# Modulated input made k tile by k tile: shift and scale of one tile at a time, four products with w_glu following; the norm's sums on TensorE

## The chip, the cores and the metric

One core of one Trainium2 chip runs the whole program. The metric is the time of one execution on the device in microseconds, and a kernel's time is the median of its runs.

## What is computed

The reference is a two-part network over 512 tokens of width 1024; the change lies at its very beginning. There a condition vector `c` gives six modulation vectors, two of which shift and scale the normalised input:

```python
mod = jax.nn.silu(c) @ w_ada[l] + b_ada[l]                      # 1024 -> 6 x 1024
sh1, sc1, gt1, sh2, sc2, gt2 = jnp.split(mod, 6, axis=-1)
h = modulate(rmsnorm(x, g_norm1[l]), sh1, sc1)                  # x_norm * g * (1 + sc1) + sh1
z = h @ w_in                                                    # all projections of the mixer
u = glu_a * jax.nn.sigmoid(glu_b)                               # the first 2 x 512 columns of z
```

After it come two causal convolutions, a chunked recurrent mixer, a mixture of 32 experts, and a second block with a delta rule, attention and two feed-forward layers.

## The kernel before

All activations are kept transposed: eight k tiles of 128 features x 512 tokens. A dense product (`dense`, L129, L132, L135) multiplies fp32 values as two rounded parts: for each of the eight k tiles it issues three matmuls of 512 columns, high x high, high x low, low x high, so 24 for one tile of 128 outputs. Weights come in `raw` tiles of 1 MB (five buffers), each with two such output tiles; ScalarE rounds them (`whi`, L105) and VectorE subtracts to get the low part (`wlo`, L106).

At the start, `ada_first` computes the shift and scale parts of `mod`. SP loads the eight tiles of `xT` and eight `raw` tiles of `w_ada`. ScalarE squares the x tiles (L1110), GpSimd adds the squares (L1112), TensorE sums over the features by one set of one-column matmuls (L172), and 13 small VectorE steps (`rsqrt_steps`, L150 to L165) give the norm, which TensorE broadcasts (L196). VectorE multiplies the rows of `w_ada` with the entries of silu(c) and accumulates (L1077, L1079); TensorE sums the accumulators over the partitions (L1085). GpSimd multiplies x with the norm (L1131). Then the mixer makes each tile's high part (L1386, ScalarE) and low part (L1387, L1389, VectorE). `glu_conv` runs eight products with the four `w_glu` tiles, and the next part of the modulation, `ada(2)`, streams beside it: eight tiles of 512 KB through the pool `ada` of three buffers (L1097), accumulated in `acc`. After `w_glu` comes the narrow product with `w_if` (L277).

Each engine runs its instructions in order. Inside a `manual_schedule` the listed engines keep the order of the code; elsewhere a scheduler sets it. SP's order, that of the loads, is the code's here, where `merge` interleaves `glu_conv` and `ada(2)`. A load into a buffer still in use waits in SP's queue, and the loads behind it wait too.

## Time and profile before

| | |
|---|---|
| median of three runs | 2391.74 us (2390.03 to 2392.57) |
| the profiled execution: time, span | 2389.36 us, 2387.6 us |
| TensorE matmuls busy | 2269.1 us (95% of the span) |
| VectorE busy | 1698.2 us (71%) |
| ScalarE busy | 1179.8 us (49%) |
| GpSimd busy | 205.7 us (9%) |
| read from HBM | 365.85 MB |

A busy share is an average over the whole span; the ends of matmuls are modelled, so two of them may be shown to overlap. An engine's idle time before an instruction is listed with what ended it. What matters for a change at the start is where TensorE is idle there, and whether it is ever idle later.

### The profile page before, as it was taken

Reading aid. Unit: us, or ns where it says so; the run is one execution under the profiler, and the core shown is the slowest. Engines: PE = TensorE matmul, PEld = TensorE weight load, DVE = VectorE, ACT = ScalarE, POOL = GpSimd, SP = SyncE. Lnnn points to the kernel's source line nnn. Section 1 sums busy time; section 2 is a strip of 40 time slices with the busy share of each in tenths; the row PEclk is TensorE's granted clock in tenths of the full one; section 3 lists DMA queues with packets and bytes.
Section 4 is the critical chain, followed back from the end, with each engine's and each line's share of the span. In section 5 each row is a group of like instructions: output and inputs, shape, how many; then the busy total and the mean of one; then the engine's idle time right before and its main releaser. Section 6 shows DMA issues by size and latency. Waiting matters only on the chain.

```text
span 2387.6 us, 30070 instructions
## 1 busy us (share of the span) xinstructions
PE 2269.1 (95%) x11062; PEld 1816.8 (76%) x11062; DVE 1698.2 (71%) x2931; ACT 1179.8 (49%) x1921; POOL 205.7 (9%) x283
## 2 busy tenths in 40 slices
PE   3999999799999999969999999999999999999997
PEld 2787788687677676636888887888888888888886
DVE  7698874688888888756677766763765766763763
ACT  2253443578777777755444424442444664432441
POOL 4000100001001001311233310000000000000000
PEclk9999999899999999979999999999999999999998
DMA  7634143279999999961111112223222212223220
GB/s 280 245 115 141 36 150 124 96 270 364 360 363 360 361 364 362 380 265 54 54 54 36 36 54 89 95 72 125 92 72 75 89 54 89 95 73 124 95 73 36
DMA packets 63302, 374.26 MB, mean 157 GB/s; under 512 B 8880, under 2 KB 9264, under 8 KB 25264
## 3 DMA queue, kind: packets, MB, share of 16 engines
q1 hardware_dynamic: 60048, 367.97, 41.7%
q0 software_dynamic: 2816, 4.20, 0.5%
q8 instruction: 88, 1.44, 0.2%
q14 instruction: 62, 0.51, 0.1%
q10 hardware_dynamic: 288, 0.14, 0.0%
HBM read 365.85 MB, written 11.67 MB: 158 GB/s over the span
## 4 chain that ended last, share of the span: by engine, by line
PE 47%; DVE 4%; POOL 2%; ACT 2%; issue 1%; DMA 1%; SPq 0%; DVEq 0%; POOLq 0%; ACTq 0%
PE mm L135 13%; PE mm L132 13%; PE mm L129 13%; PE wk L1045 1%; POOL blk_x L712 1%; POOL blk_t L710 1%; PE wk L743 1%; PE wk L748 1%; ACT act L1012 0%; DMA act<-yd 0%; POOL act L714 0%; PE wk L993 0%; DVE act L303 0%; PE wk L1029 0%; PE wk L1994 0%
## 5 line engine op out<-in xcount | busy, mean ns | idle before, releaser
L105 ACT CAST whi<-raw 128x1024 fp32r<-128x1024 f32 (+1 forms) x597 | 596.5, 1020 | 656.9 <-PE mm L132 526.2
L106 DVE TENSOR_TENSOR wlo<-raw,whi 128x1024 fp32r<-128x1024 f32 (+1 forms) x596 | 697.7, 1185 | 211.9 <-ACT whi L105 205.2
L129 PE MATMUL mm<-act,whi 128*128 128x512 f32 x1968 | 781.0, 398 | 2.1 <-DVE res L472 1.2
L132 PE MATMUL mm<-act,whi 128*128 128x512 f32 x1968 | 779.3, 396 | 2.7 <-DVE act L1389 2.3
L135 PE MATMUL mm<-act,wlo 128*128 128x512 f32 x1968 | 779.0, 396 | 0.3 <-DVE wlo L106 0.3
L132 PEld LDWEIGHTS mm<-act,whi 128*128 128x128 f32 x1968 | 371.6, 189 | 81.9 <-DVE act L1389 4.7
L129 PEld LDWEIGHTS mm<-act,whi 128*128 128x128 f32 x1968 | 371.8, 189 | 80.4 <-ACT whi L105 2.7
L135 PEld LDWEIGHTS mm<-act,wlo 128*128 128x128 f32 x1968 | 371.3, 189 | 79.3 <-issue 3.4
L303 DVE SCALAR_TENSOR_TENSOR act<-act,vec,act 128x511 f32<-128x511 f32 (+2 forms) x272 | 205.1, 756 | 19.0 <-ACT act L298 12.4
L1770 PE MATMUL gu<-whi,act 128*128 128x512 f32 x520 | 174.0, 421 | 0.2 <-ACT whi L105 0.2
L1770 PE MATMUL gu<-wlo,act 128*128 128x512 f32 x456 | 152.7, 416 | 9.4 <-DVE wlo L106 5.7
L105 ACT CAST act<-act 128x512 fp32r<-128x512 f32 (+1 forms) x96 | 52.8, 557 | 150.1 <-DVE act L349 93.6
L340 DVE TENSOR_TENSOR act<-mm,act 128x512 f32<-128x512 f32 x88 | 60.4, 688 | 84.4 <-PE mm L135 84.0
L1770 PEld LDWEIGHTS gu<-whi,act 128*128 128x128 f32 x520 | 93.6, 189 | 30.2 <-issue 13.2
L1770 PEld LDWEIGHTS gu<-wlo,act 128*128 128x128 f32 x456 | 76.7, 188 | 49.7 <-DVE wlo L106 39.6
L1844 POOL DMA_INDIRECT yd<-y,lst x32 | 68.6, 2144 | 484.5 <-DVE y L1843 414.6
L1747 PEld LDWEIGHTS xg<-s,act 128*128 128x128 f32 x576 | 85.9, 194 | 12.1 <-ACT act L113 2.0
L1747 PE MATMUL xg<-s,act 128*128 128x256 f32 x576 | 89.0, 287 | 1.9 <-DVE s L1732 1.9
L1181 DVE SCALAR_TENSOR_TENSOR act<-act,dw_half,act 128x482 f32<-128x482 f32 (+14 forms) x120 | 89.0, 743 | 0.5
L106 DVE TENSOR_TENSOR act<-act,act 128x512 fp32r<-128x512 f32 (+1 forms) x96 | 58.8, 612 | 42.3 <-ACT act L105 42.3
L300 ACT ACTIVATE act<-act,vec 128x512 f32<-128x512 f32 x96 | 78.0, 814 | 12.1 <-DVE act L340 8.4
L1770 PE MATMUL py<-whi,act 128*128 128x512 f32 x168 | 66.7, 478 | 2.7 <-DVE y L1843 2.7
(551 smaller groups left out, 2570.5 us busy)
## 6 DMA issues: line engine op xcount, KB each, us to landing
raw<-in_w_gu_dram SPq DMA_DIRECT2D x128, 1024.0 KB, 7.4
raw<-in_w_dn_dram SPq DMA_DIRECT2D x64, 1024.0 KB, 7.2
raw<-in_f_up_dram SPq DMA_DIRECT2D x44, 1024.0 KB, 4.8
raw<-in_f_dn_dram SPq DMA_DIRECT2D x32, 704.0 KB, 4.1
ada<-in_w_ada_dram SPq DMA_DIRECT2D x32, 512.0 KB, 5.2
raw<-in_a_h_dram SPq DMA_DIRECT2D x16, 1024.0 KB, 4.9
raw<-in_w_ada_dram SPq DMA_DIRECT2D x8, 1024.0 KB, 9.6
raw<-in_w_glu_dram SPq DMA_DIRECT2D x4, 1024.0 KB, 7.5
```

The source lines that it names most:

```text
L105: self.nc.scalar.copy(out=hi, in_=src)
L106: self.nc.vector.tensor_tensor(out=lo, in0=src, in1=hi.bitcast(F32), op=ALU.subtract)
L129: mm(out=p, lhsT=wh[:, s], rhs=xh, start=first and k == 0, stop=False)
L132: mm(out=p, lhsT=wh[:, s], rhs=xl, start=False, stop=False)
L135: mm(out=p, lhsT=wl[:, s], rhs=xh, start=False, stop=last and k == n - 1)
L300: nc.scalar.activation(out=y, in_=z, func=ACTF.Identity, scale=taps[n - 1], bias=bias)
L303: nc.vector.scalar_tensor_tensor(out=y[:, s:], in0=z[:, :T - s], scalar=taps[j], in1=y[:, s:], op0=ALU.mult, op1=ALU.add)
L340: nc.vector.tensor_tensor(out=z, in0=p, in1=rb, op=ALU.mult)
L1181: nc.vector.scalar_tensor_tensor(out=y[:, s:], in0=u[:, :T - s], scalar=taps[:, j, i:i + 1], in1=y[:, s:], op0=ALU.mult, op1=ALU.add)
L1747: nc.tensor.matmul(out=p[:, :n * r], lhsT=hT[k // 4][i][e][:, (k % 4) * 128:(k % 4) * 128 + 128], rhs=s[:, i, :n * r], start=i + e == 0, s ...
L1770: self.nc.tensor.matmul(out=o, lhsT=x, rhs=y[:, i * T:(i + 1) * T], start=first and p == 0, stop=last and p == len(ps) - 1)
L1844: nc.gpsimd.indirect_dma_start(out=self.yd, out_offset=bass.IndirectOffsetOnAxis(ap=rows[:r], axis=0), in_=y[:r], in_offset=None, bounds_c ...
```

## The change

`start` takes the place of `ada_first` and of the first four products. The first two parts of `w_ada` are laid out by output tile: one `raw` tile holds what is needed for shift and scale of one k tile. For tiles 0 to 2 (`ADA_PE`) the sums are 16 one-column matmuls each (L1156); for tiles 3 to 7 VectorE multiplies with a broadcast of silu(c) and sums (L1163; `ISA` with 128x1 alone reads out a sum). The broadcast `acc_182` comes from eight matmuls with the identity (L1123). The norm's sums are one set of one-column matmuls per square, without GpSimd's additions. A k tile is scaled by the norm (L1171, GpSimd from tile 2 on), modulated (L1172) and split, and the four products with `w_glu` tiles 0 and 1 take their 12 matmuls of this k tile. Four PSUM tiles accumulate at once, and the fourth split weight lies in two buffers of the pool `ada`. `w_glu` tiles 2 and 3 follow as before. TensorE, VectorE, ScalarE and SP keep the order of the code in `start`.

```diff
@@ -1068,6 +1068,8 @@
 
 M1, M2 = 1.1, 1.1
 
+ADA_PE = 3
+
...
@@ -1101,72 +1103,124 @@
-    def ada_first(self, w_ada, cs, b_ada, mod, g_norm1, g1, xs, ts):
...
+    def start(self, c, cs, mod, x):
+
+
+        nc = self.nc
+        mm = nc.tensor.matmul
+        g1 = self.const("gain1", [128, KD])
+        sc = lambda t: t.rearrange("p (a k) -> p a k", k=KD)[:, 0:2]
+        xs = []
+        for k in range(KD):
+            t = self.res()
+            nc.sync.dma_start(out=t, in_=c["xT"][k])
+            xs.append(t)
+
+        cb, rb = self.tl("ada", "acc", [128, 1024], F32, 1), self.act()
+        for j in range(2):
+            p = self.wk_ps()
+            for i in range(4):
+                mm(out=p[:, i * 128:(i + 1) * 128], lhsT=cs[:, 4 * j + i:4 * j + i + 1].to_broadcast([128, 128]),
+                   rhs=self.ident, start=True, stop=True)
+            nc.scalar.copy(out=cb[:, j * T:(j + 1) * T], in_=p)
+        p = self.wk_ps()
+        for k in range(KD):
             sq = self.act()
+            nc.scalar.activation(out=sq, in_=xs[k], func=ACTF.Square)
+            self.colsums(p, sq, k == 0, k == KD - 1)
         r = self.small([128, NT], tag="r")
+        for _ in self.rsqrt_steps(r, p[:, :NT], NT, 1.0 / D, EPS):
+            pass
+        pb = self.bcast_cols(r)
+        nc.scalar.copy(out=rb, in_=pb)
+        ws, ps = [], [self.mm_ps() for _ in range(3)] + [self.wk_ps()]
+        raws = {0: self.raw(c["w_ada0"](0), 2048)}
+
+        def glu(i):
+            w = self.raw(c["w_glu"](i), 2048)
+            for e in range(2):
+                s = w[:, e * 1024:(e + 1) * 1024]
+                if len(ws) < 3:
+                    ws.append(self.split_w(s, 1024))
+                else:
+                    ws.append(tuple(self.tl("ada", "ada", [128, 1024], F32R) for _ in range(2)))
+                    self.split(*ws[-1], s)
+
+        def columns(k):
+
+            w = raws.pop(k)
+            if k < ADA_PE:
+                p = self.wk_ps()
+                for e in range(2):
+                    for j in range(KD):
+                        mm(out=p[:, e:e + 1], lhsT=w[:, e * 1024 + j * 128:e * 1024 + j * 128 + 128], rhs=cs[:, j:j + 1],
+                           start=j == 0, stop=j == KD - 1)
+                p = p[:, 0:2]
+            else:
+                p = self.small([128, 2])
+                for e in range(2):
+                    v = w[:, e * 1024:(e + 1) * 1024]
+                    nc.vector.tensor_tensor_reduce(out=v, in0=v, in1=cb, scale=1.0, scalar=0.0, op0=ALU.mult,
+                                                   op1=ALU.add, accum_out=p[:, e:e + 1])
+            nc.vector.tensor_tensor(out=sc(mod)[:, :, k], in0=p, in1=sc(c["b_ada"])[:, :, k], op=ALU.add)
+            nc.vector.scalar_tensor_tensor(out=g1[:, k:k + 1], in0=mod[:, 8 + k:9 + k], scalar=1.0,
+                                           in1=c["g_norm1"][:, k:k + 1], op0=ALU.add, op1=ALU.mult)
+
+        def operand(k):
+            t, hi, lo = self.act(), self.act(F32R), self.act(F32R)
+            (nc.vector if k < 2 else nc.gpsimd).tensor_tensor(out=t, in0=xs[k], in1=rb, op=ALU.mult)
+            nc.scalar.activation(out=t, in_=t, func=ACTF.Identity, scale=g1[:, k:k + 1], bias=mod[:, k:k + 1])
+            self.split(hi, lo, t)
+            x.append((hi, lo))
+
+        def products(k, n):
+            for i in n:
+                self.dense(ps[i], ws[i], [x[k]], first=k == 0, last=k == KD - 1, off=k * 128)
+
+        glu(0)
+        columns(0)
+        operand(0)
+        for k in (1, 2):
+            raws[k] = self.raw(c["w_ada0"](k), 2048)
+        columns(1)
+        operand(1)
+        glu(1)
+        columns(2)
+        operand(2)
+        for k in range(3, KD):
+            raws[k] = self.raw(c["w_ada0"](k), 2048)
         for k in range(KD):
+            products(k, range(4))
+            if k + 3 < KD:
+                columns(k + 3)
+                operand(k + 3)
+        return ps
...
-    def glu_conv(self, w, wab, x, us):
+    def glu_conv(self, ps, wab, x, us):
+
 
         nc = self.nc
         for i in range(4):
-            if i:
+            zs = ps[2 * i:2 * i + 2]
+            if not zs:
                 w = self.raw(wab(i), 2048)
-            zs = []
-            for e in range(2):
-                wp = self.split_w(w[:, e * 1024:(e + 1) * 1024], 1024)
-                p = self.mm_ps()
-                self.dense(p, wp, x)
-                zs.append(p)
+                for e in range(2):
+                    wp = self.split_w(w[:, e * 1024:(e + 1) * 1024], 1024)
+                    p = self.mm_ps()
+                    self.dense(p, wp, x)
+                    zs.append(p)
             sg = self.act()
             nc.scalar.activation(out=sg, in_=zs[1], func=ACTF.Tanh, scale=0.5)
             u = self.act()
             nc.vector.scalar_tensor_tensor(out=u, in0=sg, scalar=1.0, in1=zs[0], op0=ALU.add, op1=ALU.mult)
             us.append(u)
-            yield
+            if i:
+                yield
 
...
@@ -1369,27 +1423,14 @@
         nc.scalar.activation(out=cs, in_=c["c"], func=ACTF.Silu)
         mod = self.const("mod", [128, 48])
         ada = lambda *parts: self.ada_part(c["w_ada"], parts, cs, c["b_ada"], mod)
-        xs, ts, x = [], [], []
...
-        with self.tc.manual_schedule(engines={SP}):
...
-            with self.tc.manual_schedule(engines={DVE}):
-                self.ada_first(c["w_ada"], cs, c["b_ada"], mod, c["g_norm1"], g1, xs, ts)
-            w = self.raw(c["w_glu"](0), 2048)
+        x = []
+        E = mybir.EngineType
+        with self.tc.manual_schedule(engines={E.SP}):
+            with self.tc.manual_schedule(engines={E.PE, E.DVE, E.Activation}):
+                ps = self.start(c, cs, mod, x)
             self.load_consts()
-            for k in range(KD):
...
-                nc.vector.tensor_tensor(out=lo, in0=ts[k], in1=hi.bitcast(F32), op=ALU.subtract)
-                x.append((hi, lo))
             us = []
-            merge((self.glu_conv(w, c["w_glu"], x, us), 4), (ada(2), 9))
+            merge((self.glu_conv(ps, c["w_glu"], x, us), 3), (ada(2), 9))
...
-    ada = i["w_ada"][0].reshape(4, 2, 128, 6, 1024).transpose(3, 0, 2, 1, 4).reshape(6, 4, 128, 2048)
+    ada = i["w_ada"][0].reshape(4, 2, 128, 6, 1024).transpose(3, 0, 2, 1, 4).reshape(6, 4, 128, 2048)[2:]
+
+    a0 = i["w_ada"][0][:, :2048].reshape(8, 128, 2, 8, 128)
+    ada0 = np.concatenate([a0.transpose(3, 1, 2, 0, 4)[:ADA_PE].reshape(-1, 128, 2048),
+                           a0.transpose(3, 4, 2, 0, 1)[ADA_PE:].reshape(-1, 128, 2048)])
```

What the diff alone does not show is the order on the engines. A name in brackets is what an instruction waits for (DMAHW: a load; the others: an engine).

TensorE, from the norm's broadcast (L196) to the first products, before (first row of each set; `act_282` and `act_283` hold the two halves of the shift):

```order
L196 MATMUL wk_250<-ident,r[4]dt.float_20_210 128x128 [waits DVE_49]
L1085 MATMUL wk_273<-ones,acc_211 128x1 [waits DVE_49]
L1085 MATMUL wk_310<-ones,act_282 128x1 [waits DVE_49]
L1085 MATMUL wk_316<-ones,act_283 128x1 [waits DVE_49]
L129 MATMUL mm_378<-act_327,whi_374 128x512 [waits Activation_49]
L129 MATMUL mm_407<-act_327,whi_403 128x512
L132 MATMUL mm_378<-act_328,whi_374 128x512 [waits DVE_49]
```

And now (`wk_290`, `wk_320`, `wk_356` are the columns of tiles 0, 1 and 2, 16 matmuls each; `mm_581` is the first product with `w_glu` tile 2; between the L132 and the L135 row stand the other 93 matmuls of the four products):

```order
L172 MATMUL wk_196<-ones,act_239 128x1 [waits Activation_49]
L196 MATMUL wk_268<-ident,r[4]dt.float_24_245 128x128 [waits DVE_49]
L1156 MATMUL wk_290<-cs,raw_278 128x1 [waits DMAHW1_49]
L1156 MATMUL wk_320<-cs,raw_316 128x1 [waits DMAHW3_49,PE_49]
L1156 MATMUL wk_356<-cs,raw_318 128x1 [waits DMAHW4_49,PE_49]
L129 MATMUL mm_274<-act_310,whi_282 128x512 [waits Activation_49]
L132 MATMUL mm_274<-act_311,whi_282 128x512 [waits DVE_49]
L135 MATMUL wk_277<-act_506,ada_353 128x512
L129 MATMUL mm_581<-act_310,whi_577 128x512 [waits Activation_49]
```

The sums of the modulation for three tiles now stand between the broadcast and the first product, which needs only tile 0; behind the four products w_glu tile 2 comes at once.

VectorE, where the low parts of x are made, before:

```order
L1089 TENSOR_TENSOR mod<-wk_310,vec 128x4 [waits PE_49]
L106 TENSOR_TENSOR wlo_375<-raw_323,whi_374 128x1024 [waits DMAHW1_49,Activation_49]
L1089 TENSOR_TENSOR mod<-wk_316,vec 128x4 [waits PE_49]
L1387 TENSOR_SCALAR act_257<-act_257,gain_161,mod 128x512 [waits Activation_49]
L106 TENSOR_TENSOR wlo_404<-raw_323,whi_403 128x1024
L1389 TENSOR_TENSOR act_328<-act_257,act_327 128x512 [waits DVE_49]
L1077 TENSOR_SCALAR acc_367<-ada_368,cs 128x1024 [waits DMAHW4_49]
L1387 TENSOR_SCALAR act_259<-act_259,gain_161,mod 128x512 [waits Activation_49]
```

And now (`act_377` and `act_411` are the low parts of tiles 2 and 3, `raw_382` and `raw_384` the weights for tiles 3 and 4, `acc_182` the broadcast c):

```order
L1165 TENSOR_TENSOR mod<-wk_356,vec 128x2 [waits PE_49]
L1166 SCALAR_TENSOR_TENSOR gain_165<-mod,vec 128x1 [waits DVE_49]
L106 TENSOR_TENSOR act_377<-act_375,act_376 128x512 [waits Activation_49]
L1163 ISA raw_382,small[2]dt.float_69_404<-raw_382,acc_182 128x1024 [waits DMAHW6_49,DMAHW1_49]
L1163 ISA small[2]dt.float_69_404 128x1
L1163 ISA raw_382,small[2]dt.float_69_404<-raw_382,acc_182 128x1024
L1163 ISA small[2]dt.float_69_404 128x1
L1165 TENSOR_TENSOR mod<-small[2]dt.float_69_404,vec 128x2 [waits DVE_49]
L1166 SCALAR_TENSOR_TENSOR gain_165<-mod,vec 128x1 [waits DVE_49]
L106 TENSOR_TENSOR act_411<-act_409,act_410 128x512 [waits Activation_49]
L1163 ISA raw_384,small[2]dt.float_73_428<-raw_384,acc_182 128x1024 [waits DMAHW7_49,DMAHW3_49]
```

Before, all of shift and scale stood ahead of the first low part; now the reductions of tile k+1 stand behind the low part of tile k, which waits for ScalarE.

SP's queue, the loads of `w_glu` and of `ada(2)`, before (the two loads of constants behind the first row are left out):

```order
L93 DMA raw_323<-in_w_glu_dram 128x2048 [waits DMAHW4_49,DVE_49]
L1097 DMA ada_368<-in_w_ada_dram 128x1024
L1097 DMA ada_371<-in_w_ada_dram 128x1024 [waits DMAHW5_49]
L1097 DMA ada_436<-in_w_ada_dram 128x1024 [waits DMAHW6_49]
L1097 DMA ada_439<-in_w_ada_dram 128x1024 [waits DMAHW7_49,DMAHW4_49,DVE_49]
L93 DMA raw_442<-in_w_glu_dram 128x2048 [waits DMAHW0_49]
L1097 DMA ada_506<-in_w_ada_dram 128x1024 [waits DMAHW5_49,DMAHW1_49,DVE_49]
L1097 DMA ada_509<-in_w_ada_dram 128x1024 [waits DMAHW6_49,DMAHW2_49,DVE_49]
L93 DMA raw_512<-in_w_glu_dram 128x2048 [waits DMAHW3_49]
```

And now, from the weights of tile 6 on (constants left out again; `raw_575` is `w_glu` tile 2, `ada_552` to `ada_572` are the first five tiles of `ada(2)`):

```order
L93 DMA raw_388<-in_w_ada_dram 128x2048 [waits DMAHW2_49,DVE_49]
L93 DMA raw_390<-in_w_ada_dram 128x2048 [waits DMAHW5_49,DVE_49]
L1099 DMA ada_552<-in_w_ada_dram 128x1024
L1099 DMA ada_555<-in_w_ada_dram 128x1024 [waits DMAHW6_49,DMAHW5_49,DVE_49]
L1099 DMA ada_566<-in_w_ada_dram 128x1024 [waits DMAHW7_49,PE_49]
L1099 DMA ada_569<-in_w_ada_dram 128x1024 [waits DMAHW6_49,DMAHW0_49,DVE_49]
L1099 DMA ada_572<-in_w_ada_dram 128x1024 [waits DMAHW1_49,PE_49]
L93 DMA raw_575<-in_w_glu_dram 128x2048 [waits DMAHW2_49]
```

The load of w_glu tile 2 now stands behind five tiles of `ada(2)`, two of which wait for TensorE; before, tiles 1 and 2 stood behind waits for loads and VectorE alone.

## Rows read from the trace of the kernel before

**Rows 1.** The profile's 40 slices of the span (59.7 us each): TensorE's busy share in tenths.

```profile
PE   3999999799999999969999999999999999999997
```

**Rows 2.** The windows, one stretch of 10 us: busy time and instructions of TensorE, its weight loads, VectorE, ScalarE and GpSimd, then TensorE's granted clock, the DMA share and GB/s.

```profile
30.00:40.00 10.00, 0.33 (x2) 0.24 (x2) 9.96 (x8) 1.99 (x2) 10.00 (x7) 1.00 0.80 293
```

**Rows 3.** The list of TensorE's waits from 60 to 428 us, all of it: engine, tile and line, what it waited for, then us in total, times, and the longest.

```profile
PE wk L1345 <- ACT act L1342: 1.2, 1, 1.2
PE mm L132 <- DVE act L106: 0.4, 1, 0.4
PE wk L1246 <- DVE act L1242: 0.4, 1, 0.4
```

**Rows 4.** The timeline of TensorE from the start to 101 us, in parts: start us, duration us, line, operation, tiles, shapes, records (an fp32 matmul leaves two), and the idle time before with what ended it.

```profile
17.20 1.87 PE L172 MATMUL wk<-ones,act 128*128 128x1 f32 x8 [17.20 <-POOL act L1112]
25.05 2.07 PE L196 MATMUL wk<-ident,r[4]dt.float 128*128 128x128 f32 x8 [5.99 <-DVE r[4]dt.float L165]
26.92 3.41 PE L1085 MATMUL wk<-ones,acc 128*128 128x1 f32 x16
43.92 3.57 PE L1085 MATMUL wk<-ones,act 128*128 128x1 f32 x16 [13.59 <-DVE act L1079]
47.36 1.20 PE L129 MATMUL mm<-act,whi 128*128 128x512 f32 x2
...
51.81 0.63 PE L135 MATMUL mm<-act,wlo 128*128 128x512 f32 x1
...
57.24 0.40 PE L129 MATMUL mm<-act,whi 128*128 128x512 f32 x1
...
70.93 1.84 PE L1085 MATMUL wk<-ones,acc 128*128 128x1 f32 x16
72.63 0.47 PE L135 MATMUL mm<-act,wlo 128*128 128x512 f32 x1
...
77.83 0.40 PE L129 MATMUL mm<-act,whi 128*128 128x512 f32 x1
...
100.24 0.39 PE L277 MATMUL mm<-act,whi 128*16 128x512 f32 x1
```

**Rows 5.** The same timeline around 320 us.

```profile
319.85 1.84 PE L1085 MATMUL wk<-ones,acc 128*128 128x1 f32 x16
321.55 3.00 PE L1513 MATMUL wk<-vec,mod 128*128 128x36 f32 x16
324.36 0.77 PE L129 MATMUL mm<-act,whi 128*128 128x512 f32 x1
324.93 0.63 PE L132 MATMUL mm<-act,whi 128*128 128x512 f32 x1
325.36 0.63 PE L135 MATMUL mm<-act,wlo 128*128 128x512 f32 x1
...
329.13 0.39 PE L132 MATMUL mm<-act,whi 128*128 128x512 f32 x1
```

**Rows 6.** The windows, one stretch of 1 us at 323 us; columns as in rows 2.

```profile
323.00:324.00 1.00, 1.00 (x7) 1.00 (x6) 1.00 (x2) 1.00 (x3) 0.00 (x0) 0.50 0.83 254
```

**Rows 7.** VectorE's groups of instructions from 0 to 120 us, shapes kept apart: count, busy us, mean ns of one, idle time before.

```profile
L106 DVE TENSOR_TENSOR wlo<-raw,whi 128x1024 fp32r<-128x1024 f32 x12 | 14.6, 1222 | 7.3 <-ACT whi L105 7.3
L1079 DVE SCALAR_TENSOR_TENSOR acc<-raw,cs,acc 128x1024 f32<-128x1024 f32 x7 | 10.7, 1533 | 0.1
...
L1077 DVE TENSOR_SCALAR acc<-ada,cs 128x1024 f32<-128x1024 f32 x2 | 1.5, 748 | 0.5 <-DMA ada<-in_w_ada_dram 0.5
```

**Rows 8.** VectorE's groups over the whole span: the reductions of two operands (L1000) and the instruction that reads out their sum.

```profile
L1000 DVE CUSTOM_DVE_ANT_0 act<-wk,distM 128x256 f32<-128x256 f32 x48 | 17.6, 416 | 0.1
...
L1000 DVE DVE_READ_ACCUMULATOR2_ANT ll[4]dt.float<- 128x1 f32 x64 | 5.3, 83 | 0.0
...
L1000 DVE CUSTOM_DVE_ANT_0 act<-wk,distM 128x128 f32<-128x128 f32 x16 | 3.7, 282 | 0.0
```

**Rows 9.** The costliest groups of the page: the rounding of an activation tile and the subtraction that makes its low part.

```profile
L105 ACT CAST act<-act 128x512 fp32r<-128x512 f32 (+1 forms) x96 | 52.8, 557 | 150.1 <-DVE act L349 93.6
...
L106 DVE TENSOR_TENSOR act<-act,act 128x512 fp32r<-128x512 f32 (+1 forms) x96 | 58.8, 612 | 42.3 <-ACT act L105 42.3
```

**Rows 10.** The timeline, in parts: ScalarE at the start and at 46 us, and TensorE in the final norm at the end of the kernel.

```profile
2.62 0.21 ACT L1369 ACTIVATE cs<-vec 128x8 f32<-128x8 f32 x1 [0.54 <-DMA vec<-in_vec_dram]
...
7.17 3.29 ACT L1110 ACTIVATE act<-res 128x512 f32<-128x512 f32 x5 [1.29 <-DMA res<-in_xT_dram]
...
46.09 3.63 ACT L1386 ACTIVATE act<-act,mod,gain 128x512 fp32r<-128x512 f32 x5 [11.12 <-DVE mod L1089]
...
2372.96 1.28 PE L172 MATMUL wk<-ones,act 128*128 128x1 f32 x8 [0.66 <-ACT act L181]
2376.67 2.07 PE L196 MATMUL wk<-ident,rt[4]dt.float 128*128 128x128 f32 x8 [2.44 <-DVE rt[4]dt.float L165]
```

**Rows 11.** The timeline of SP's queue and ScalarE at 51 to 57 us: the issue of w_glu tile 1 and the cast that waited for it.

```profile
50.95 0.43 SPq L93 DMA_DIRECT2D raw<-in_w_glu_dram  x1
...
57.17 1.05 ACT L105 CAST whi<-raw 128x1024 fp32r<-128x1024 f32 x1 [7.44 <-DMA raw<-in_w_glu_dram]
```

**Rows 12.** DMA issues from 0 to 110 us: tile and tensor, queue, count, KB each, median us from issue to landing.

```profile
raw<-in_w_ada_dram SPq DMA_DIRECT2D x8, 1024.0 KB, 9.6
raw<-in_w_glu_dram SPq DMA_DIRECT2D x4, 1024.0 KB, 7.5
```

50 lines of the change are left out of this document (2 added, 48 removed).

## The prediction

> **What bounds the kernel now.** I read the slices of the span first: TensorE is at 9 tenths nearly everywhere, and the first slice of 60 us has 3 [rows 1]. So the question is what TensorE does there and whether a shift at the start reaches the end. The list of TensorE's waits answers the second: between 60 and 428 us it waits for 2.0 us in all [rows 3], so whatever moves the dense stream at 60 us moves everything behind it. The first follows from its timeline [rows 4]. Narrow fp32 matmuls (each leaves two records) run at 17 us (column sums), 25 us (broadcast of the norm), 27 us and 44 us (sums of the modulation), and the first product with w_glu starts at 47.36 us. Between 30 and 40 us TensorE works for 0.33 us while VectorE is at 9.96 of 10: the modulation's sums bound the start [rows 2]. From 47.36 us on the first four products (96 matmuls) run, w_glu tile 2 begins at 77.83 us and w_if (L277) at 100.24 us. That last time is my yardstick: in both kernels the same work precedes it, and the order behind it is nearly the same.
>
> **TensorE's clock at the start.** In the cold prefix 16 records of a one-column sum take 3.57 us (0.223 each), at 70.93 us the same 16 take 1.84 [rows 4]. A 512-column matmul is shown with 0.63 us at 51.81 and with 0.40 at 57.24. Where the granted clock is 0.50, from 323 us [rows 6], the same matmul has that 0.63 and stands 0.43 us from the next [rows 5]; at full rate it is 0.233 (22.41 us from 77.83 to 100.24 for 96). So all of the prefix runs at 1.2 GHz, though the windows print a granted clock of 1.00 there [rows 2]. At 319.85 us the trace shows what narrow matmuls do to a clock that is up: sums of one column and products of 36 columns follow each other without a gap, TensorE is busy throughout, and the clock falls inside them, before 323 us. It rises only after 4.7 us of 512-column matmuls (324.36 to 329.1) [rows 5]. The new prefix consists of narrow matmuls, so I cost it at 1.2 GHz.
>
> The Trainium skill ("TensorE: Matmul & The Clock Gate", section "What's actually happening") says that the throttled state is the default and that activity of the engine releases it, by how busy it has been. Read plainly, a prefix that keeps TensorE issuing without pause would run at 2.4 GHz; the trace does not agree for narrow matmuls. What this would make of the time is the second rival.
>
> **The norm.** The new ScalarE order puts two copies of the broadcast c ahead of the squares. The broadcast is two sets of four matmuls of the form that took 2.07 us [rows 4]; c is ready at 2.83 us [rows 10], and after the sets and ScalarE's copy of the second the squares begin near 7.5. Eight squares at 0.66 (3.29 for five) [rows 10] end near 12.8. But each square now has four sums on TensorE, 8 records, 1.87 us alone, 1.78 in a row: 8 x 1.78 = 14.2 from 8.2 us gives 22.5 (before: GpSimd's additions, then one set, ending at 19.1). The 13 small VectorE steps now run uninterrupted: 2.43 us from sums to broadcast at the end of the kernel [rows 10], instead of 6.0 between other work [rows 4]. So the broadcast starts at 25.0 us, as before: the slower sums and the faster steps cancel.
>
> **The modulation.** It then takes 2.07 us, and `columns(0..2)` follow on TensorE, all three ahead of the first product, 16 matmuls or 32 records each: 32 x 0.223 = 7.1 us, three times, 21.4 us. The first product starts at 25.05 + 2.07 + 21.4 = 48.5 us, 1.1 later than before. The bounds are 3.7 us each (the 2.4 GHz row, -10 us) and 7.1; I take the latter, since the same form in the same place has it. GpSimd's multiplications of tiles 2 to 7 and the splits of w_glu lie under these 21 us.
>
> From tile 3 on the sums of a tile are on VectorE, which runs in order: two reductions, two small steps, then the wait for ScalarE's modulated tile and its rounding, then the subtraction, then the next tile. The reduction of 1024 columns is not in the trace. The same instruction takes 0.282 us at 128 columns and 0.416 at 256 [rows 8], 1.05 ns a column, which gives an estimate of 1.22, equal to the two-input operation of that size (1.222) [rows 7]. Per tile: 2 x 1.22, 2 x 0.08 for reading the sums [rows 8], 2 x 0.19 small steps (2.43 over 13), 0.73 for the ScalarE scaling (3.63 for five) [rows 10], 0.56 for rounding and 0.61 for the subtraction [rows 9], and some 0.26 for the hand-overs: 5.14 us. Tile 2 needs its columns (48.5) and the same without the reductions, 2.6: 51.1. Five more tiles: 25.7. Ahead of tile 7's gain stands the first step of the next modulation part, 0.75 [rows 7]. Tile 7 is ready at 77.6 us. TensorE needs 12 x 0.233 = 2.8 us a tile, or 5.1 at 1.2 GHz, and so waits for this chain from about tile 5 on. The bounds of a reduction are 0.75 (the one-input operation) and 1.53 (the two-input one beside GpSimd's work in this prefix) [rows 7]; 0.31 up or 0.47 down, ten times, is +3.1 or -4.7 us. The last 11 matmuls then take 2.6 or 4.7 us by the clock, which bursts of 2.8 in 5.1 us leave open: the four products end between 80.2 and 82.3 us; I take 81.3.
>
> **The wait that is new.** On SP's queue w_glu tile 2 stands behind five loads of the next modulation part. They stream through a pool of three buffers, and two of these now hold the split of the fourth w_glu column until the last product. The first load waits for nothing, the second for VectorE, the third and fifth for TensorE, that is for the end of the four products; everything on SP's queue stands behind them. Before, w_glu tiles 1 to 3 were issued at 51, 54 and 62 us, long before use. Now: 81.4 third load, three issues at 0.43, tile 2 issued at 82.7. It lands 7.5 us later (median of this group) [rows 12]: 90.2. ScalarE's cast takes 1.05 [rows 11]: TensorE goes on at 91.3, after 10 us of nothing. The bounds are 6.2 us (issued at 50.95, used at 57.17 [rows 11]) and 9.6 (the group with the longest queue): 8.7 to 12.1 us of wait. VectorE's half of the split takes 1.22, of which the first two matmuls hide 0.85: 0.4 more. After 10 idle us the clock is down: 4.7 us at 1.2 GHz hold 11 matmuls at 0.427 instead of 0.233, 2.1 more. w_glu tile 3 is issued behind three more loads near 90 us and lands by 99, ahead of its use at 105; that costs nothing, and it is the next to be late.
>
> **The sum**, against the profiled execution (span 2387.6, time 2389.36). After TensorE goes on: 91.3 + 0.4 + 96 x 0.233 (22.4) + 2.1 + 1.7 for the sums of the next part (70.93 to 72.63, in both kernels ahead of L277) = 117.9, against 100.24: 17.7 us later. What the change removes from VectorE (16 half-width steps and 8 modulations) buys nothing behind 60 us, where TensorE waits for 2.0 us in all. The median of the runs shown is 2391.74, 2.4 above the profiled one; 2391.74 + 17.7 = 2409.4. I take 2409.
>
> **Rivals.**
> 1. The load of w_glu tile 2 is not late: the queue is not held up, or something else covers it. For it: SP issues in order, but nothing in the trace of before waits in this way. Against it: the order of the loads and their waits. Then the 10, the 0.4 and the 2.1 go, the pause is about 1.3 us, and the yardstick is at 106.7: +6.5 us, 2398.
> 2. The clock rises in the prefix. Sums cost 0.95 a set and end with the squares at 13.8, the norm's broadcast starts at 16.2 and takes 1.0, the three columns take 3.6 each: 28.2 instead of 48.5. The chain on VectorE goes with them: 57.3 for tile 7, the products end at 60, TensorE goes on at 70, and the yardstick is at 97.6, 2.6 us earlier than before: 2389, no longer slower. It decides on TensorE alone: my forecast turns into no change where the three columns take less than half as long. For it: TensorE issues without pause from 8 us on. Against it: rows 5 and 6, and the 5.2 us from 25.05 to 30.3 that ended at 0.22 a record. The page named above reads this way.
> 3. The chain per tile is longer, or the clock stays down after tile 2 as well (96 instead of 11 matmuls, 16 us): 2420 or more.
> 4. That the change does not do what it says is excluded by its order, shown above: the products stand tile by tile.
>
> **How the numbers follow.** My forecast has 0.83, rival 1 0.06, rival 2 0.06, rival 3 0.04, and 0.01 is left for a gain that I do not see. What can be told from no change by a measurement is 0.2%, 4.8 us: 2387 to 2396.5. Slower holds the forecast, rivals 1 and 3, less what of the lower ends falls under 2396.5: 0.89. Same holds rival 2 and that rest: 0.08; faster 0.03. The range: the products' end moves by -5 to +4 us, the pause by -1.3 to +2.1, and the steps behind may give back 1 us of the 2.0. Together about -8 and +7 when they do not all fall together: 2401 to 2416. It takes in neither rival 2 nor 3; 1 lies just below, and I reach to 2400.
>
> **What would show it.** In the new profile: narrow matmuls at 0.22 us a record up to 48 us; first product at 47 to 50; steps of about 5.1 us from tile to tile on VectorE from 51 us on; TensorE idle for 9 to 12 us near 81 us, ended by ScalarE's cast and that by the load of w_glu; L277 near 118 us. A first product near 28 us, a reduction far from 1.22 us, or a load of w_glu issued before the products end would make it wrong.

## The result: 0.84% slower, and the profile after

The changed kernel takes 2411.36 us (median of four runs, 2408.68 to 2413.30) against 2391.69 us for the kernel before beside it: a ratio of 1.0084, 95% interval 1.0072 to 1.0096, so it is slower. The profiled spans are 2409.2 and 2387.6 us. One execution below, the profiled one of e8, ran at a granted clock of 0.55 and took 3765 us, so its time and its profile are not used.

Line numbers from here on are those of the changed kernel; rows of an experiment carry those of its own kernel. "Part 2" is `ada(2)` (the third ada load of the expectations below), "part 3" is `ada(3)` (the fourth).

The slices of the page, as in [rows 1]:

```profile
PE   8799999799999999969899999999999999999998
```

The first slice now has 8 tenths instead of 3: TensorE is at work from 3 us on, from 7.6 us with the norm's sums. The second has 7: a hole that was not there.

TensorE's timeline, first to last column: start, duration, engine and line, operation, tiles, and in brackets the idle time ahead with what ended it:

```profile
7.62 12.28 PE L172 MATMUL wk<-ones,act 128*128 128x1 f32 x64 [1.21 <-ACT act L1129]
22.33 2.07 PE L196 MATMUL wk<-ident,r[4]dt.float 128*128 128x128 f32 x8 [2.43 <-DVE r[4]dt.float L165]
24.20 20.48 PE L1156 MATMUL wk<-cs,raw 128*128 128x1 f32 x96
44.54 0.77 PE L129 MATMUL mm<-act,whi 128*128 128x512 f32 x1
...
73.19 0.50 PE L129 MATMUL mm<-act,whi 128*128 128x512 f32 x1 [1.94 <-ACT act L105]
...
88.54 0.79 PE L129 MATMUL mm<-act,whi 128*128 128x512 f32 x1 [10.25 <-ACT whi L105]
...
114.03 1.84 PE L1087 MATMUL wk<-ones,acc 128*128 128x1 f32 x16
115.73 0.39 PE L277 MATMUL mm<-act,whi 128*16 128x512 f32 x1
```

Against [rows 4], the first product starts at 44.54 us (before 47.36) and L277 at 115.73 (before 100.24). In between stands the idle time of 10.25 us that the prediction names, ended by ScalarE's cast of a w_glu tile. SP's queue shows why:

```profile
47.38 31.99 SPq L1099 DMA_DIRECT2D ada<-in_w_ada_dram  x5
79.42 0.42 SPq L93 DMA_DIRECT2D raw<-in_w_glu_dram  x1
```

Five loads of part 2 take 32 us to be issued, since they wait for buffers, and w_glu tile 2 stands behind them; it is issued after the last of the four products, whose last three matmuls run from 77.27 to 78.29 us.

VectorE from the low part of one tile to that of the next:

```profile
62.70 0.69 DVE L106 TENSOR_TENSOR act<-act,act 128x512 fp32r<-128x512 f32 x1 [1.59 <-ACT act L105]
63.31 1.22 DVE L1163 CUSTOM_DVE_ANT_0 raw<-raw,acc 128x1024 f32<-128x1024 f32 x1
...
64.45 1.22 DVE L1163 CUSTOM_DVE_ANT_0 raw<-raw,acc 128x1024 f32<-128x1024 f32 x1
...
65.72 0.16 DVE L1165 TENSOR_TENSOR mod<-small[2]dt.float,vec 128x2 f32<-128x2 f32 x1
65.91 0.16 DVE L1166 SCALAR_TENSOR_TENSOR gain<-mod,vec 128x1 f32<-128x1 f32 x1
67.67 0.69 DVE L106 TENSOR_TENSOR act<-act,act 128x512 fp32r<-128x512 f32 x1 [1.59 <-ACT act L105]
```

One reduction of 1024 columns takes 1.22 us, and the step from tile to tile is 4.97 us.

TensorE's waits between 60 and 428 us, the list that is 2.0 us long in [rows 3]:

```profile
PE mm L129 <- ACT whi L105: 10.2, 1, 10.2
PE mm L129 <- ACT act L105: 3.3, 2, 1.9
PE wk L1330 <- ACT act L1320: 1.9, 1, 1.9
PE mm L132 <- DVE act L106: 1.9, 5, 0.8
PE mm L129 <- ACT act L1320: 1.6, 2, 1.3
...
PE wk L1285 <- issue: 1.1, 1, 1.1
```

Only the first entry was foreseen, and the second and the L106 one belong to the chain. The waits at L1330, for L1320 and at L1285 lie *behind* L277, where the prediction has nothing. They are part of a second loss: L277 is 15.5 us late, the transposes of the mixer's heads (L1399; L1345 before) are 23.8 us late (241.70 against 217.85), the router's first sums (L1554; L1513 before) as well, and of that 21.6 are left at the end.

What VectorE does in that stretch:

```profile
109.47 1.22 DVE L106 TENSOR_TENSOR wlo<-raw,whi 128x1024 fp32r<-128x1024 f32 x1 [5.13 <-ACT whi L105]
115.91 0.17 DVE L1091 TENSOR_TENSOR mod<-wk,vec 128x8 f32<-128x8 f32 x1 [5.21 <-PE wk L1087]
115.99 0.75 DVE L1079 TENSOR_SCALAR acc<-ada,cs 128x1024 f32<-128x1024 f32 x1
...
122.78 0.17 DVE L1275 TENSOR_SCALAR ll[4, 4]dt.float<-act 128x16 f32<-128x16 f32 x1
122.86 1.27 DVE L1081 SCALAR_TENSOR_TENSOR acc<-ada,cs,acc 128x1024 f32<-128x1024 f32 x1
125.73 1.28 DVE L1081 SCALAR_TENSOR_TENSOR acc<-ada,cs,acc 128x1024 f32<-128x1024 f32 x1 [1.59 <-DMA ada<-in_w_ada_dram]
126.93 0.17 DVE L540 TENSOR_SCALAR ll[4, 4]dt.float<-ll[4, 4]dt.float 128x16 f32<-128x16 f32 x1
127.24 1.28 DVE L1081 SCALAR_TENSOR_TENSOR acc<-ada,cs,acc 128x1024 f32<-128x1024 f32 x1
128.44 0.25 DVE L542 RECIPROCAL ll[4, 4]dt.float<-ll[4, 4]dt.float 128x16 f32<-128x16 f32 x1
```

VectorE idles for 5.13 and 5.21 us, and the second wait is for part 2's sums on TensorE (L1087), which stand behind the w_glu passes. Then the eight steps of part 3 (L1079 and L1081) follow, in between the small steps of the gates (L1275, L540, L542). In the kernel before, part 3 ran between 74.67 and 100.59 us, in a stretch where VectorE had time, and the gates were not interrupted.

### The profile page after: what moved, and what is told of

It is laid out like the page before. It is cut to its first block, busy times and chain, and to the rows that moved or that the text cites. A ratio compares the mean times of both kernels' runs of the same rounds, so it can differ in the third digit from the quotient of the medians.

```text
span 2409.2 us, 30342 instructions
## 1 busy us (share of the span) xinstructions
PE 2303.1 (96%) x11198; PEld 1847.1 (77%) x11198; DVE 1683.9 (70%) x2933; ACT 1185.3 (49%) x1931; POOL 191.4 (8%) x274
## 4 chain that ended last, share of the span: by engine, by line
PE 46%; DVE 4%; POOL 2%; ACT 2%; issue 1%; DMA 0%; SPq 0%; DVEq 0%; POOLq 0%; ACTq 0%
PE mm L135 13%; PE mm L132 13%; PE mm L129 13%; PE wk L1045 1%; POOL blk_x L712 1%; POOL blk_t L710 1%; PE wk L743 1%; PE wk L748 1%; ACT act L1012 0%; POOL act L714 0%; PE wk L993 0%; DVE act L303 0%; PE wk L1029 0%; PE wk L2035 0%; PE po L780 0%
## 5 line engine op out<-in xcount | busy, mean ns | idle before, releaser
L106 DVE TENSOR_TENSOR wlo<-raw,whi 128x1024 fp32r<-128x1024 f32 (+1 forms) x595 | 697.8, 1187 | 220.1 <-ACT whi L105 213.5
L132 PE MATMUL mm<-act,whi 128*128 128x512 f32 x1960 | 779.0, 398 | 1.9 <-DVE act L106 1.9
L135 PE MATMUL mm<-act,wlo 128*128 128x512 f32 x1960 | 778.6, 397 | 0.4 <-DVE wlo L106 0.3
L132 PEld LDWEIGHTS mm<-act,whi 128*128 128x128 f32 x1960 | 372.0, 190 | 80.5 <-DVE act L106 3.9
L135 PEld LDWEIGHTS mm<-act,wlo 128*128 128x128 f32 x1960 | 371.2, 189 | 80.4 <-issue 3.3
L105 ACT CAST act<-act 128x512 fp32r<-128x512 f32 (+1 forms) x104 | 57.8, 562 | 150.4 <-DVE act L349 93.7
L106 DVE TENSOR_TENSOR act<-act,act 128x512 fp32r<-128x512 f32 (+1 forms) x104 | 65.0, 625 | 53.3 <-ACT act L105 53.3
```

The costliest lines, as they stand in the source:

```text
L105: self.nc.scalar.copy(out=hi, in_=src)
L106: self.nc.vector.tensor_tensor(out=lo, in0=src, in1=hi.bitcast(F32), op=ALU.subtract)
L132: mm(out=p, lhsT=wh[:, s], rhs=xl, start=False, stop=False)
L135: mm(out=p, lhsT=wl[:, s], rhs=xh, start=False, stop=last and k == n - 1)
```

## Experiments

All are edits of the changed kernel; each was run beside the kernel before (2390.2 to 2390.7 us). In the diffs `...` marks lines left out.

### The pause: w_glu's last two tiles loaded first (e1_glu_first)

```diff
...
-                w = self.raw(wab(i), 2048)
+                w = early.pop(0)
...
             self.load_consts()
             us = []
-            merge((self.glu_conv(ps, c["w_glu"], x, us), 3), (ada(2), 9))
+            early = [self.raw(c["w_glu"](i), 2048) for i in (2, 3)]
+            merge((self.glu_conv(ps, c["w_glu"], x, us, early), 3), (ada(2), 9))
```

> Tiles 2 and 3 of w_glu are loaded right behind the constants, ahead of the third ada load that SP waits on. Theory (the pause of 10.25 us at 88.5 us is the late load and nothing else): the pause shrinks to under 1 us, the clock stays up in the w_glu passes behind it (some 2 us more), L277 starts at 103 to 104 instead of 115.7. Of the 6 to 8 us that are lost between 120 and 150 us nothing comes back, since the gate steps keep their order: 2411 - 12 = about 2399 us, within 2396 to 2402. Rival (the load is late only because the products are, and something else stands right behind it): a new wait of several us takes the place of the pause, 2405 us or more.

Measured: 2399.39 us, ratio to before 1.0038 (1.0024 to 1.0053), 12.0 us less than the changed kernel. TensorE's timeline:

```profile
102.54 1.84 PE L1087 MATMUL wk<-ones,acc 128*128 128x1 f32 x16
104.24 0.39 PE L277 MATMUL mm<-act,whi 128*16 128x512 f32 x1
```

No wait for a w_glu tile is left. L277 is at 104.24 us, 11.5 us earlier, and the loss behind it stays: L277 is 4.0 us later than in the kernel before, L1399 10.0 us. The late load is the cause of the pause, and 12.0 us are what it cost.

### The chain: the next reductions ahead of the low part (e3_reduce_ahead)

```diff
...
-            products(k, range(4))
             if k + 3 < KD:
                 columns(k + 3)
-                operand(k + 3)
+                low()
+                low = operand(k + 3)
+            elif low:
+                low()
+                low = None
+            products(k, range(4))
```

`operand` now returns the subtraction of the low part instead of doing it; for tiles 0 and 1 the caller does it at once.

> On VectorE the reductions of tile k+1 stand ahead of the low part of tile k, so that they no longer wait behind it. Theory (from the first product to the last the chain reduction, scale, cast, low part of one tile after the other binds, 4.97 us a tile): VectorE then has two reductions (2.6 us) and a low part (0.75) a tile, about 3.6 us, and TensorE's own columns of the first tiles and the four products take over; the products end at 69 to 71 instead of 77.8 us; the third ada load and the late load of w_glu move along with them, so the pause stays near 10 us: 2411 - 8 = about 2403 us (2401 to 2406). Rival (TensorE or a load binds there): products end within 2 us of before, 2409 to 2412 us.

Measured: 2405.53 us, 1.0070 (1.0053 to 1.0087). Two low parts on VectorE and TensorE's end of the products and next wait:

```profile
50.94 0.68 DVE L1175 TENSOR_TENSOR act<-act,act 128x512 fp32r<-128x512 f32 x1
...
54.22 0.69 DVE L1175 TENSOR_TENSOR act<-act,act 128x512 fp32r<-128x512 f32 x1
...
67.95 0.40 PE L135 MATMUL wk<-act,ada 128*128 128x512 f32 x1
80.81 0.80 PE L129 MATMUL mm<-act,whi 128*128 128x512 f32 x1 [12.46 <-ACT whi L105]
```

A tile takes 3.28 us instead of 4.97, the products end at 68.3 us instead of 78.3, and the pause moves with them and becomes 12.46 us. VectorE's chain bound the four products. The time falls by 5.8 us, less than these 10.0, since the pause is 2.2 us longer.

### Both (e7_both_waits)

> Tiles 2 and 3 of w_glu loaded first, and the reductions of tile k+1 ahead of the low part of tile k; the fourth ada load is as in the changed kernel. If the two gains add up (11.9 and 5.9 us as measured alone): 2411 - 18 = about 2393 us (2391 to 2395), L277 at 96 to 98 us. If the reductions' gain was only that the loads came earlier, as with w_glu first: 2397 to 2400 us.

Measured: 2389.57 us, 0.9996 (0.9986 to 1.0006): as fast as the kernel before. L277 is at 92.34 us, 7.9 *earlier* than before, but L1399 only 1.5 earlier. Without the pause the change gains 7.9 us up to L277 and loses 6.4 behind it. The gain of 21.8 us over the changed kernel is 4 us more than the two edits gave alone (12.0 and 5.8), so the expected range was missed on the good side; the longer pause, which held back part of e3's gain, does not arise here.

### The norm's sums (e4_gpsimd_sums)

```diff
-            self.colsums(p, sq, k == 0, k == KD - 1)
+            if k:
+                nc.gpsimd.tensor_tensor(out=sq, in0=sq, in1=total, op=ALU.add)
+            total = sq
+        self.colsums(p, total)
```

> The norm's squares are added up on GpSimd again and only the last tile is summed over the partitions on TensorE, as in the kernel before; the rest is as changed. Theory (the sums on TensorE neither cost nor give, since in both kernels they end at 19 to 20 us): rsqrt within 1 us of before, 2410 us within 2408.5 to 2412.5. Rival (the 64 one-column matmuls hold the columns up, or keep something else waiting): 2406 us or less. Other rival (GpSimd's adds, of which each waits for the one before, would have ended later): 2414 us or more.

Measured: 2411.77 us, 1.0087 (1.0071 to 1.0104): no difference. The sums begin at 17.73 us instead of 7.62, and the broadcast of the norm starts at 22.02 us instead of 22.33.

### TensorE's clock in the prefix (e6_dense_burst)

```diff
         glu(0)
+        burn = self.wk_ps()
+        for _ in range(14):
+            mm(out=burn, lhsT=ws[0][0][:, 0:128], rhs=ws[0][0][:, 0:T], start=True, stop=True)
         columns(0)
```

> 14 matmuls of 512 columns without use (some 5 us) stand on TensorE ahead of the one-column matmuls of the first tiles. Theory (one-column matmuls cannot hold the clock up, as in the 323 us stretch of the kernel before): the clock rises in the burst, the columns start near 0.115 us each and are back at 0.213 within a few us; the first product comes 2 to 5 us later than 44.5. Rival (any work keeps the clock once it is up): all 96 columns at 0.115, 11 us instead of 20.5, and the first product at about 40.

Measured: 2414.37 us in one run. Timeline, and then three stretches, with TensorE's busy time behind the length and the granted clock third from the end:

```profile
25.66 5.89 PE L1183 MATMUL wk<-whi 128*128 128x512 f32 x14 [1.62 <-ACT whi L105]
31.39 17.80 PE L1156 MATMUL wk<-cs,raw 128*128 128x1 f32 x96
49.04 0.78 PE L129 MATMUL mm<-act,whi 128*128 128x512 f32 x1
```

```profile
30.00:34.00 4.00, 4.00 (x30) 3.65 (x28) 0.00 (x0) 0.00 (x0) 4.00 (x4) 0.89 0.73 262
34.00:40.00 6.00, 6.00 (x32) 6.00 (x31) 1.61 (x4) 1.43 (x2) 0.51 (x3) 0.53 0.50 175
40.00:49.00 9.00, 9.00 (x44) 9.00 (x44) 3.98 (x6) 3.33 (x4) 0.00 (x0) 0.50 0.31 117
```

The burst raises the clock (0.89 from 30 to 34 us), and it is down to 0.50 again while the columns follow each other without a pause: TensorE is busy for the whole of all three stretches. All 96 take 17.80 us instead of 20.48, the first product starts 4.5 us later. The theory held, and the second rival of the prediction is out. The Trainium skill ("TensorE: Matmul & The Clock Gate", section "What's actually happening"), read as the prediction reads it, would have kept the clock up; this trace does not agree for one-column matmuls.

### All tiles reduced on VectorE (e5_all_on_vector, e15_vector_both)

```diff
-ADA_PE = 3
+ADA_PE = 0
```

> All eight tiles' shift and scale are reduced on VectorE, none on TensorE: the 20.5 us of one-column matmuls ahead of the first product are gone, and three more pairs of reductions stand in VectorE's chain of 5.0 us a tile. First product at about 31 instead of 44.5 us. Theory (VectorE's chain then sets the pace): tile 7 ready at 68, products end at 71 instead of 77.8, 2411 - 6 = about 2405 us (2402 to 2408). Rival (TensorE, half idle, stays at 1.2 GHz, where the twelve matmuls of a tile take 5.1 us, or the w_ada0 loads come too late): products end at 75 to 78, 2408 to 2412 us.

Measured: 2416.56 us, 1.0107 (1.0090 to 1.0124). The first product starts at 40.43 us, not at 31, and the last ends at 83.8. GpSimd's products with the norm and VectorE's first reductions, beside them:

```profile
26.97 11.29 POOL L1171 TENSOR_TENSOR act<-res,act 128x512 f32<-128x512 f32 x6 [21.26 <-ACT act L1135]
...
31.44 2.28 DVE L1163 CUSTOM_DVE_ANT_0 raw<-raw,acc 128x1024 f32<-128x1024 f32 x1
...
35.96 1.10 DVE L1165 TENSOR_TENSOR mod<-small[2]dt.float,vec 128x2 f32<-128x2 f32 x1
...
41.02 1.22 DVE L1163 CUSTOM_DVE_ANT_0 raw<-raw,acc 128x1024 f32<-128x1024 f32 x1
```

A reduction takes 2.28 us while GpSimd works and 1.22 after it. So the 20.5 us of columns that are gone from TensorE bring the first product only 4 us forward (6 us, if one allows for the norm's broadcast, which started 1.9 us later in this profile), and three more tiles in VectorE's chain of 5 us cost more than that. Neither theory had this. The same edit together with the two of e7:

> All reductions on VectorE, the reductions of tile k+1 ahead of the low part of tile k, and tiles 2 and 3 of w_glu loaded first. If the removed columns come out of the time: products end at 63 to 65 us, about 4 to 5 us ahead of the kernel that has the other two edits (2389.6), 2385 us (2382 to 2388), less than the kernel before. If TensorE's clock stays down between the tiles (5.1 us for a tile's twelve matmuls) or loads come late: 2388 to 2393 us.

Measured: 2394.52 us, 1.0014 (1.0004 to 1.0023), 5.0 us more than e7: taking the columns away does not make the time shorter.

### The loss behind L277: part 3 put behind the gates (e2_gates_alone)

```diff
+        cs3 = self.const("cs3", [128, KD])
+        nc.vector.scalar_tensor_tensor(out=cs3, in0=self.ml_nu.rearrange("p n h -> p (n h)")[:, :KD], scalar=0.0, in1=cs,
+                                       op0=ALU.mult, op1=ALU.add)
+        ada3 = self.ada_part(c["w_ada"], (3,), cs3, c["b_ada"], mod)
...
-        merge((chain(*proj), 12), (ada(3), 9), fill=(conv, 9))
+        merge((chain(*proj), 12), (ada3, 9), fill=(conv, 9))
```

> The products of the third ada load are made from a copy of the conditioning vector that is ready only behind the LRU gates, so that VectorE's accumulation steps of 1.28 us no longer stand between the small gate steps. Theory (these steps, put between the gates, are the loss behind 115 us): the gates run without a break, TensorE's waits at L1330 and the fall of its clock at 142 to 146 us go, 2411 - 6 = about 2405 us (2402 to 2407). Rival (the loss there has to do with TensorE's clock or the loads, not with this order): 2409 to 2412 us. The pause of 10.25 us stays in both.

Measured: 2415.33 us, 1.0111 (1.0095 to 1.0128): *slower* than the changed kernel. The gates run without a break (17.7 us from L277 to the last of their transposes, before 16.8, changed 24.1), and yet the heads' transposes come hardly sooner after L277, and the next stretch is 5.4 us longer: from L277 to the router's sums it takes 233.3 us, in the changed kernel 229.7. The break in the gates alone is not the loss, since without it at least as much is lost behind them. With w_glu first and the reductions ahead as well (e8_all_three):

> The three edits together: w_glu's tiles 2 and 3 loaded first, the reductions ahead of the low parts, the third ada load's steps behind the gates. If the three losses are separate: products end at 70 us, no pause, gates without a break, 2411 - 8 - 12 - 6 = about 2385 us (2382 to 2389), which is less than the kernel before. If the constants' load or the third ada load, now later than the gates, takes the place of one of them: 2390 to 2398 us.

Measured: 2394.52 us, 1.0020 (1.0011 to 1.0030), 5.0 us more than e7 without this edit, and above the first of the two ranges.

### Part 3 made earlier (e9_second_acc, e10_acc_glu_reduce, e12_acc_in_place)

```diff
-            acc = self.tl("ada", "acc", [128, 1024], F32, 1)
+            acc = self.tl("ada", "acc", [128, 1024], F32, 2)
...
-            self.pool("act", 41, ctx=ph)
+            self.pool("act", 39, ctx=ph)
```

> The accumulator of the VectorE ada loads gets a second buffer (4 KB a partition, taken from the pool of activation tiles, 39 instead of 41). Theory (the fourth ada load's eight steps wait, while VectorE idles from 104 to 116 us, for the accumulator that the third load's sums on TensorE read at 114 us behind the w_glu passes; they then fall into a stretch in which VectorE is full): most of these steps now run before 116 us, the gates' last step comes 4 to 6 us earlier, 2411 - 5 = about 2406 us (2404 to 2408). Rival (VectorE's work there is not what TensorE lacks, or the smaller pool costs as much): 2410 to 2413 us. The pause of 10.25 us stays.

> As the kernel with w_glu first and the reductions ahead, and with a second accumulator besides. If the three losses are separate: 2393 - 5 = about 2388 us (2385 to 2391), at or below the kernel before. If the second accumulator gives nothing once w_glu comes first (the third ada load is late anyway there): 2392 to 2395 us.

The second run has the edits of e1 and e3 as well. Measured: 2424.47 us, 1.0136 (1.0119 to 1.0153), and 2403.94 us, 1.0052 (1.0036 to 1.0069). In e9 the gates are done 6.7 us earlier than in the changed kernel, a little more than expected, but the modulation parts behind part 3 also start earlier (at 138.5 us in e9), and the attention part of the heads then shows a new wait:

```profile
PE wk L1373 <- DVE act L1364: 12.7, 1, 12.7
```

Both lie above every range that was expected, by 11 and 9 us. Whether the earlier steps or the two missing activation tiles make the new wait, these two runs can't tell. e12 has neither edit:

```diff
-            acc = self.tl("ada", "acc", [128, 1024], F32, 1)
+            acc = None if i == 2 else self.tl("ada", "acc", [128, 1024], F32, 1)
             for k in range(KD):
                 w = self.tl("ada", "ada", [128, 1024])
+                acc = acc or w
```

> The third ada load is accumulated in place, in the buffer of its own first tile, so that the one accumulator is free for the fourth load from the start and the later loads keep their places; no pool is made smaller. Theory (the fourth load's steps stood among the gates only because they waited for the accumulator until 114 us): five of the eight steps now run before the gates, the gates end about 5 us earlier as they did with a second accumulator, and this time nothing behind them takes it back: 2411 - 5 = about 2406 us (2404 to 2408). Rival (whatever the order, these 9.7 us of VectorE come back as waits of TensorE in the full stretch behind, as where they were moved behind the gates): 2410 to 2414 us.

Measured: 2416.81 us, 1.0110 (1.0093 to 1.0127). SP, then TensorE:

```profile
47.07 38.31 SPq L1100 DMA_DIRECT2D ada<-in_w_ada_dram  x5
85.43 0.42 SPq L93 DMA_DIRECT2D raw<-in_w_glu_dram  x1
...
95.44 0.79 PE L129 MATMUL mm<-act,whi 128*128 128x512 f32 x1 [17.29 <-ACT whi L105]
```

The accumulator now holds one of the three `ada` buffers, part 2's loads take 38.3 us to be issued, w_glu tile 2 goes out 6 us later and the pause is 17.29 us. That is the queue's mechanism once more, and it hides whatever the edit gains. Three steps fewer (five were expected) lie behind L277, and that stretch is 2.7 us shorter than in the changed kernel, but only 0.3 shorter than in e1, which has all of them.

### What the thirteen profiles say together

The stretch from L277 to the heads' transposes, worked out for all kernels but e8 from each timeline and from the busy time of the stretch. For before and changed that row reads (length, then busy time and instruction counts of TensorE, its weight loads, VectorE, ScalarE, GpSimd, then granted clock, DMA share and GB/s):

```profile
100.24:217.85 117.61, 117.17 (x536) 92.53 (x534) 103.62 (x195) 53.25 (x85) 4.66 (x14) 1.00 0.41 143
```

```profile
115.73:241.70 125.97, 121.16 (x537) 94.52 (x537) 112.37 (x204) 50.91 (x83) 3.23 (x14) 0.97 0.46 159
```

```
                L277   ada steps  stretch  VectorE  stretch less  next stretch
                at us  in it      us       busy us  VectorE       to the router
before          100.2      9      117.6    103.6    14.0          103.7
changed         115.7     16      126.0    112.4    13.6          103.7
e1 glu first    104.2     16      123.6    112.3    11.3          103.7
e2 gates        113.5     16      124.3    112.0    12.3          109.1
e3 reduce       107.1     16      125.6    112.5    13.1          103.7
e4 norm         114.3     16      125.4    112.3    13.1          103.8
e5 vector       120.0     16      125.7    112.2    13.5          103.7
e6 burst        117.2     16      125.8    112.3    13.6          103.7
e7 both          92.3     16      124.0    112.4    11.6          103.7
e9 second acc   115.0     20      128.1    115.9    12.2          112.6
e10             95.6      23      129.3    118.2    11.1          114.2
e12 in place    122.6     13      123.2    109.4    13.9          103.7
e15              97.8     16      127.0    112.3    14.7          103.7
```

All kernels with 16 steps in the stretch are longer there than the kernel before with 9, by 6.0 to 9.4 us, and VectorE's idle time in it stays between 11 and 15 us in all thirteen. The changed kernel has seven steps more in it; VectorE is busy for 8.75 us longer, and the stretch is 8.36 us longer. By TensorE's columns these 8.36 us are 4.4 us more of idle time (4.8 against 0.4) and 4.0 us more of busy time for one record more, at a granted clock of 0.97 instead of 1.00.

Right behind the gates VectorE is all but full in both kernels (before, then changed):

```profile
117.00:162.00 45.00, 44.94 (x202) 36.43 (x203) 43.60 (x76) 24.98 (x38) 2.15 (x8) 1.00 0.30 107
140.00:185.00 45.00, 41.53 (x177) 32.67 (x177) 43.90 (x76) 23.02 (x37) 0.70 (x8) 0.96 0.28 97
```

In these 45 us VectorE works through 76 instructions in either kernel and is busy for 97% of the time. In the kernel before TensorE is busy throughout as well. In the changed kernel it has done more of its matmuls during the longer gates (109 records against 77) and now waits. So gates that end later on VectorE put off what follows them, and VectorE has no gap there to make up for it.

This is the reading that fits the rows best: the change moves 8.75 us of VectorE's work out of the stretch of the w_glu passes, where VectorE had idle time, into one where it has next to none. That these steps are the cause is argued and not shown. No kernel with the steps taken out altogether was run. The eight kernels with 16 steps, e2 left aside, differ by 3.4 us among themselves (123.6 to 127.0), so the 123.2 us of e12 with 13 steps do not stand out. In e2, e9 and e10 TensorE has 548, 500 and 500 records in the stretch instead of 537: work has moved across its end, and their lengths compare with the others only together with the last column. The spread of 3.6 us in the fifth column stays unexplained.

## Why the prediction was right, and where it was not

The second point below goes by these rows, the norm's sums on TensorE in two parts:

```profile
7.62 1.83 PE L172 MATMUL wk<-ones,act 128*128 128x1 f32 x15 [1.21 <-ACT act L1129]
9.32 10.59 PE L172 MATMUL wk<-ones,act 128*128 128x1 f32 x49
```

- **The total**: 2409 us was predicted and 2411.36 measured, and for the predicted reason in the main. But in the profiled execution 15.5 us stand at L277 (predicted 17.7) and some 6 us come behind it (predicted 0). Two errors of opposite sign cancelled in part, so that the total came out this close is partly luck.
- **The prefix at 1.2 GHz**: this was right for the columns, which took 0.213 us a record (0.223 in the sum); e6 shows why. It was not right for all of the norm's sums. The clock had risen while the 128-column matmuls that broadcast c ran; it was granted at 1.00 from 6.0 to 9.3 us and at 0.50 from there to 20 us, and the first 15 of the sums' 64 records took 1.83 us, the other 49 took 10.59. So the norm's broadcast started at 22.33 us instead of 25.0. With the columns' 0.9 us the first product came 4.0 us before the predicted 48.5, ahead of the 47 to 50 us that the prediction gives as its sign.
- **The norm is neutral**: this was right for the time (e4). That the slower sums and the faster steps just cancel was not: the broadcast started 2.7 us before that of the old kernel (25.05 us), since the sums ended only 0.8 us later than there, at 19.90 us, and the 13 small steps gave back 3.6 us.
- **The chain**: 5.14 us a tile were predicted and 4.97 measured, with the reduction at 1.22 us as estimated. The 0.26 us for the hand-overs came from no row; the gaps between the engines in one step add up to 0.17 us. Tile 4 took 6.1 us: VectorE waited 2.37 us for the rest of the constants, whose readers stand in its order; no term had that. Tile 7 was ready at 73.9 us (predicted 77.6), and the products ended at 78.3 (81.3). Of the two values that the prediction left open for the last matmuls nearly the higher one came, 4.4 us: from 74.28 to 77.27 us they stand 0.43 us apart, at 1.2 GHz.
- **The wait that is new**: this was right in place, cause and size, so rival 1 is out. The load was issued at 79.42 us, 1.1 after the products' end (1.4 in the sum); TensorE went on at 88.54 after 10.25 us of idle time (10). e1 takes the wait away and gets back 12.0 us; the sum has 10 + 0.4 + 2.1.
- **From the pause to L277**: it took 27.2 us, predicted 26.6.
- **"The order behind it is nearly the same", and nothing is lost there**: this step failed. The order of VectorE behind L277 was not the same: part 3, which before had all but ended by L277, was wholly behind it. The 2.0 us of waits in [rows 3] say that TensorE waited for nobody in the *old* kernel; they do not say how much room VectorE had. In the old stretch it was busy for 103.6 of 117.6 us, and for 43.6 of the 45 us behind the gates. The runs showed 8.36 us lost between L277 and the heads' transposes, of which some 6 are left at the end; that the 8.75 us of VectorE's work moved there are the cause is the best reading and not shown.
- **"What the change removes from VectorE buys nothing"**: no run tests this alone, and nothing speaks against it: VectorE is busy for 1683.9 us in all instead of 1698.2, and the kernel is slower. The other half was overlooked: work that is *displaced* on VectorE can cost time.

## What to carry to other kernels

A pass over k tiles that feeds several outputs at once holds all its weights, and any buffers lent to it, until its last tile. Follow the in-order load queue past each load that waits for such a buffer, and issue what is needed next ahead of it: here that one move is worth 12 of the 19.7 us lost. When a stage gets longer or shorter, list the background work that ran in another engine's idle time beside it, see in which stretch it now lands, and compare that engine's busy time with the length there, piece by piece: here VectorE was busy for 88% of the whole stretch, but for 97% of the part behind the gates. A short list of waits does not show whether there is room.

## What the runs showed of the hardware that was not expected

- VectorE beside GpSimd: with GpSimd on 128x512 products, reductions took 2.28 instead of 1.22 us and a two-column addition of two SBUF tiles 1.10 instead of 0.16 (e5). The Trainium skill ("GPSIMD Engine Reference", section "Specifications") lists contention between GpSimd and VectorE instructions that have two SBUF inputs; the trace agrees.
- The start isn't fully repeatable: the same 64 records of the norm's sums took 11.78 us in e2, 12.28 in the changed kernel and 13.81 in e1. In e1 all of them stand 0.21 us apart, in the changed kernel the first 15 stand 0.11 us apart, and in e2 the first 21: TensorE's clock had risen to its higher level ahead of them in some executions and not in others. The norm's broadcast started near 22.2 or near 24.2 us accordingly, so single profiles of the start compare only to 2 us.
